# A Mamba-2 scan layer in another order, and the constant under every root moved from GpSimd to VectorE

## The chip, the cores and the metric

The kernel runs on one core of one Trainium2 chip. The metric is the device time of one execution in microseconds (us); the time of a kernel is the median of its runs. In the views of the profile PE is TensorE (matmuls), PEld its weight loads, DVE VectorE, ACT ScalarE, POOL GpSimd and SP SyncE. `L1584` is line 1584 of the kernel before.

## The reference, cut to what matters

Two layers on a sequence of 256 tokens and a model width of 1024, in float32. Each layer has a feed-forward block, a mixer and a second feed-forward block, each followed by a layer norm. The mixer of the first layer is sparse attention, that of the second a Mamba-2 scan (SSD):

```python
def layer_norm(x, g, b):
    mu = jnp.mean(xf, -1, keepdims=True)
    var = jnp.mean(jnp.square(xf - mu), -1, keepdims=True)
    return (xf - mu) * lax.rsqrt(var + LN_EPS) * g + b

def ssd_mixer(x, ...):
    z, xbc, dt = jnp.split(x @ w_in, ...)
    xbc = silu(causal_conv(xbc))                      # 4 taps
    xs, b_in, c_in = jnp.split(xbc, ...)
    dt = softplus(dt + dt_bias);  a = -exp(a_log)
    y = ssd_scan(xs, dt, a, b_in, c_in)               # 2 chunks of 128 tokens, 4 groups of 8 heads
    y = (y + xs * d_skip) * silu(z)
    y = y * lax.rsqrt(mean(square(y), per group) + RMS_EPS) * norm_g
    return y @ w_out

def ssd_scan(...):                                    # per chunk and group
    cb = einsum('bclgn,bcsgn->bcgls', cm, bm)         # C times B
    y_diag = einsum(cb * decay, xdt)                  # inside a chunk
    y_off = einsum(cm, state carried from chunk 0) * exp(a_cs)
```

Attention normalises its latent in the same way (`rms_norm` over 256 columns). So there are twelve layer-norm roots (six norms, two token tiles each), two for the latent and eight in the scan.

## The kernel before, in words

**Tiles and engines.** The 256 tokens are two token tiles t = 0, 1 of 128, which are also the two chunks of the scan. Every matmul with weights is done as three (`mm3`, L545 to L548): each operand is split into a high and a low part, and high x high, high x low and low x high are summed.

**Weights.** `Weights` (L220 on) streams the weights in units of up to 128 x 1024. SyncE loads a unit into a raw buffer (L258). `make` (L322) lets ScalarE round it to its high part (L339, with a scale L337), and `lows` (L356) lets VectorE subtract that from the raw unit for the low part (L368, with a scale L365). For six units of the scan layer the low part is made by ScalarE (L345) and an adding DMA from GpSimd's queue (L346). There are ten slots: a unit can be made while `made < done + 10`, and `free` (L410) counts a unit as done. `pump(n)` (L382) issues the low parts that are due and then makes up to n units. A raw unit is loaded when an earlier one is dead (L372).

**Order.** The program runs under a manual schedule: each engine executes its instructions in the order in which the Python code issues them, and waits by semaphore for its inputs and for buffers. So the order of the calls in `ssd` (L1618 to L1714) is the order of the work in each engine's queue.

**The scan layer up to its loop (L1618 to L1658).** `z0` and `z_half` project z, the gate; `z_half(1, 1, 0)` and `z_half(1, 1, 1)` are the two halves (over k) for group 1 and token tile 1. They sum into one PSUM bank of the pair `ptr`, free two units each, and the second half ends in a SiLU on ScalarE (L1460). `soft_a` and `soft_b` compute the softplus of dt in small GpSimd instructions, up to `adt` (L1394). Eight `bc_tile` calls project B and C. Each goes into one of three PSUM banks and through `conv`: a first tap on ScalarE (L1479), three on VectorE (L1482), and a SiLU on ScalarE (L1474), which is put off: it is issued inside the next `conv`, or by `flush()`. Behind tile 5 `cumsums` multiplies `adt` with triangles (L1402 to L1404), and `decay_load` has GpSimd's queue fetch the decay rows (L1466). Four `xs_tile` calls do the same as `bc_tile` for group 0 of x. `cb(0)`, `cb(1)` (L1504) and `cb_cross` (L1497) multiply C by B inside chunk 0, inside chunk 1 and across. `x_tok` (L1543) transposes the x tiles back to tokens (L1552), which needs the SiLU of all four.

**The loop over four groups (L1661 to L1713).** Eight pieces of other work, `f[0]` to `f[7]` (x tiles of the next group, z halves, pieces of the output product, each with a pump of one unit), are laid between the steps of the group. For token tile t the steps are `diag` (matmuls with the decay matrix, L1565), `gate` (VectorE, L1576 and L1577), `square` (ScalarE with a sum, L1581), `root`, `norm` (ScalarE scales y by the root, L1588) and `y_tr` (TensorE transposes y, L1593, and it is split). `carry` (L1569) adds to tile 1 what chunk 0 hands on: two matmuls (L1571) and two VectorE instructions (L1572, L1573). Behind the loop `tail` (L706) ends the output product, fills the slots and does the layer norm.

**Roots.** `rsqrt_pool` (L532) is called by `layernorm` (L643), `latent_norm` (L1015) and `root` (L1585). GpSimd adds the constant (L536) and raises to the power -1/2 (L538). In a root-mean-square norm a VectorE instruction ahead of it divides the sum by the width (L1584, L1014); in a layer norm VectorE's statistics (L640, L642) come ahead, and two instructions per half, centering (L649) and scaling by the root (L653), behind.

Of the kernel before, what the change touches and what calls it, by code (L numbers as in the profile page):

```python
# [13 lines left out]
ALU = mybir.AluOpType  # L14
# [10 lines left out]
KVR = 256  # L25
# [5 lines left out]
ALPHA = (2.0 * DEPTH) ** 0.25  # L31
LN_EPS = 1e-5
# [392 lines left out]
def trunk_kernel(ctx: ExitStack, tc: tile.TileContext, widths, forms, x, ln_g, ln_b, wts, kvg, convp,  # L425
# [28 lines left out]
    def tiny(s, n=32):  # L454
        return wk.tile([128, n], F32, name=nm(s), tag=f"tiny{n}", bufs=14 if n == 32 else 4)
# [73 lines left out]
    dsk = consts.tile([128, SH], F32, name="dsk")  # L529
    nc.gpsimd.dma_start(dsk, bcast_rows(d_skip, 0, SH))  # L530

    def rsqrt_pool(src, eps):  # L532

        n = src.shape[1]
        e = tiny("rse")
        nc.gpsimd.tensor_scalar(e[:, :n], src, float(eps), None, op0=ALU.add)  # L536
        o = tiny("rs")
        nc.gpsimd.tensor_tensor(o[:, :n], e[:, :n], mhalf.to_broadcast([128, n]) if n > 1 else mhalf, op=ALU.pow)  # L538
        return o[:, :n]

    def split_psum(H, L, ps):
# [77 lines left out]
    def layernorm(t, acc, c, gb, store=False, rest=None, mid=None, pre=None):  # L619

        g, b = gb
        st = tiny("st")
        x_ = xs_[t]

        def add(c0, c1, a):
            nc.vector.scalar_tensor_tensor(x_[:, c0:c1], a, c / ALPHA, x_[:, c0:c1], op0=ALU.mult, op1=ALU.add)

        w = D // 2 if rest is None else D // 4
        n = D // w
        for i in range(n):
            if i * w % 512 == 0:
                add(i * w, i * w + 512, acc[i * w // 512])
            if rest is not None and i == n - 1:
                add(i * w, D, rest)
            if pre and i == n - 1:
                pre()
            nc.vector.bn_stats(st[:, i * 6:i * 6 + 6], x_[:, i * w:(i + 1) * w])  # L640
        mv = tiny("mv", 16)
        nc.vector.bn_aggr(mv[:, :2], st[:, :6 * n].rearrange("p (a b) -> p a b", b=6))  # L642
        rstd = rsqrt_pool(mv[:, 1:2], LN_EPS / ALPHA ** 2)  # L643
        if mid:
            mid()
        hs = [slice(0, 512), slice(512, D)]

        def center(sl):
            nc.vector.scalar_tensor_tensor(x_[:, sl], x_[:, sl], mv[:, 0:1], g[:, sl],  # L649
                                           op0=ALU.subtract, op1=ALU.mult)  # L650

        def scale(sl):
            nc.vector.scalar_tensor_tensor(x_[:, sl], x_[:, sl], rstd, b[:, sl], op0=ALU.mult, op1=ALU.add)  # L653
            if store:
                nc.sync.dma_start(out[0, t * 128:(t + 1) * 128, sl], x_[:, sl])

        if store:
            for sl in hs:
                center(sl)
            for sl in hs:  # L660
                scale(sl)
        else:
            for sl in hs:
                center(sl)
                scale(sl)
# [331 lines left out]
    def attention(xT, u, ln_i):  # L997
# [13 lines left out]
            nc.scalar.activation(sq, lt[t][:, :KVR], AF.Square, accum_out=ss[t][:, 0:1])  # L1011

        def latent_norm(t):
            nc.vector.tensor_scalar(ss[t][:, 1:2], ss[t][:, 0:1], 1.0 / KVR, None, op0=ALU.mult)  # L1014
            rc = rsqrt_pool(ss[t][:, 1:2], RMS_EPS)  # L1015
            ki[t] = f1("ki")
            nc.vector.tensor_copy(ki[t][:, :128].rearrange("p (a d) -> p a d", a=2),
                                  lt[t][:, KVR + IH:NA_ATTN][:, None, :].to_broadcast([128, 2, HD]))
            wi = lt[t][:, KVR:KVR + IH]
            nc.vector.tensor_scalar(wi, wi, IH ** -0.5, None, op0=ALU.mult)  # L1020
            nc.vector.tensor_scalar(lt[t][:, :KVR], lt[t][:, :KVR], rc, None, op0=ALU.mult)
# [336 lines left out]
    def ssd(xT, u, ln_i):  # L1358
# [86 lines left out]
        def z_half(g, t, i, uu):  # L1445

            if not i:
                zps[t] = ptr() if t and g == 1 else pmm()
            ps = zps[t]
            for k in range(4 * i, 4 * i + 4):  # L1450
                H, L = W.get(uu + k // 2)
                c = slice((k % 2) * 512, (k % 2 + 1) * 512)
                sl = slice(t * 128, (t + 1) * 128)
                mm3(ps, xT.H[:, k, sl], xT.L[:, k, sl], H[:, c], L[:, c], k == 0, k == DK - 1)
                if t and k % 2:
                    W.free(uu + k // 2)
            if i:
                if not t:
                    zs[g] = f4("zs")
                nc.scalar.activation(zs[g][:, t * 512:(t + 1) * 512], ps, AF.Silu)  # L1460
# [11 lines left out]
        def flush():  # L1472
            while late:
                nc.scalar.activation(*late.pop(0), AF.Silu)  # L1474
# [22 lines left out]
        def cb_cross():  # L1497
            pt = pspare(4)
            for g in range(SG):
                nc.tensor.matmul(pt[:, g * 128:(g + 1) * 128], bT[:, g * 256:g * 256 + 128],  # L1500
                                 cTt[:, g * 256 + 128:g * 256 + 256], start=True, stop=True)
            nc.scalar.copy(cbx, pt)

        def cb(t):  # L1504
            pt = pspare(4)
            for g in range(SG):
                c = slice(g * 256 + t * 128, g * 256 + (t + 1) * 128)
                nc.tensor.matmul(pt[:, g * 128:(g + 1) * 128], bT[:, c], cTt[:, c], start=True, stop=True)
            nc.vector.tensor_mul(cbm[:, t * 512:(t + 1) * 512].rearrange("p (g l) -> p g l", g=SG),
                                 pt.rearrange("p (g l) -> p g l", g=SG),  # L1510
                                 tri[:, None, :].to_broadcast([128, SG, 128]))
# [9 lines left out]
        def decay_seg(t, g, on_act=False):  # L1521

            m = M[t, g]
            for h in range(8):
                hs = slice(h * 128, (h + 1) * 128)
                a = acs[t][:, g * 8 + h:g * 8 + h + 1]
                if on_act:
                    nc.scalar.activation(m[:, hs], m[:, hs], AF.Relu, bias=a, scale=-1.0)
                else:
                    nc.vector.tensor_scalar(m[:, hs], m[:, hs], a, 0.0, op0=ALU.subtract, op1=ALU.min)  # L1530
# [50 lines left out]
            nc.scalar.activation(xd[t], y[t], AF.Square, accum_out=ss[t][:, 0:1])  # L1581

        def root(t):
            nc.vector.tensor_scalar(ss[t][:, 1:2], ss[t][:, 0:1], 1.0 / 512, None, op0=ALU.mult)  # L1584
            ss[t] = rsqrt_pool(ss[t][:, 1:2], RMS_EPS)  # L1585

        def norm(t):
            nc.scalar.activation(y[t], y[t], AF.Copy, scale=ss[t])  # L1588
# [42 lines left out]
        s11()  # L1631
        W.pump(1)
        soft_b()
        z_half(1, 1, 0, u + 6)
        W.pump(2)
        uz = u + 6
        for i in range(8):
# [5 lines left out]
        u += 18  # L1643
        for i in range(4):
            xs_tile(0, i, u + i)
            if i == 0:
                cb_cross()
                cb(0)
                cb(1)
        decay_seg(0, 0)  # L1650
        z_half(1, 1, 1, uz)
        flush()
        x_tok(0, 0)
        x_tok(1, 0)
        decay_seg(1, 0)
# [5 lines left out]
        for g in range(SG):  # L1661
            if g < 2:
                f = [lambda i=i: xs_tile(g + 1, i, u + i) for i in range(4)]
                f += [lambda t=t, i=i: (z_half(g + 2, t, i, u + 4), W.pump(1)) for t in range(2) for i in range(2)]
            elif g == 2:
                x3 = [lambda i=i: xs_tile(3, i, u + 2 * i) for i in range(4)]
                o0 = [lambda i=i: out_piece(i, u + 2 * i + 1) for i in range(4)]
                f = [x3[0], x3[1], o0[0], x3[2], o0[1], x3[3], o0[2], o0[3]]
            else:
                f = [lambda i=i: out_piece(4 + i, u + i) for i in range(6)]  # L1670
            f[0]()
            if g:
                x_tok(0, g)
                x_tok(1, g)
            else:
                decay_cb(0, 0)
                decay_cb(1, 0)
            x_end(g)
            f[1]()
            f[2]()  # L1680
            py[0] = diag(0, g)
            gate(0, g, py[0])
            if g < 3:
                decay_load(0, g + 1)
            f[3]()
            carry(g)
            square(0)
            root(0)
            py[1] = diag(1, g)
            gate(1, g, py[1])  # L1690
            if g < 3:
                decay_load(1, g + 1)
            f[4]()
            square(1)
            root(1)
            norm(0)
            if g < 3:
                decay_seg(0, g + 1)
            f[5]()
            y_tr(0, g)  # L1700
            norm(1)
            if g < 3:
                decay_seg(1, g + 1)
                f[6]()
                flush()
                y_tr(1, g)
                decay_exp(0, g + 1)
                decay_exp(1, g + 1)
                f[7]()
                decay_cb(0, g + 1)  # L1710
                decay_cb(1, g + 1)
                W.lows()
                u += 8  # L1713
# [56 lines left out]
```

## Time and profile before

| | |
|---|---|
| time, median of 3 runs | 1024.61 us (1024.01 to 1026.11) |
| the profiled execution's own time | 1024.18 us |
| its span, first to last instruction | 1022.2 us |
| TensorE busy | 1006.5 us, 98% |
| VectorE busy | 904.0 us, 88% |
| ScalarE busy | 654.4 us, 64% |
| GpSimd busy | 110.5 us, 11% |
| HBM read, over the span | 193.48 MB, 190 GB/s |

The scan layer's own work begins at about 644 us and its loop runs from about 709 to 820 us. A row of the timeline gives the start, the length, the engine and line, the operation, what it writes and reads, a count where equal instructions follow each other, and in brackets how long the engine stood idle before and whose work ended that. A row of waits gives who waited for whom, the total, the times and the longest. A row by stretch gives for each engine the busy time and, in brackets, the instructions, then the clock granted to TensorE, the DMA share and the rate. The lines themselves stand in the prediction.

### The profile page before, as it was taken

How to read it: one execution, taken by the hardware profiler on the slowest of the kernel's cores; microseconds unless marked ns; L12 is line 12 of the kernel's file. 1: busy time of each engine (PE TensorE's matmuls, PEld its weight loads, DVE VectorE, ACT ScalarE, POOL GpSimd, SP SyncE). 2: the span in 40 equal slices, each digit the busy share in tenths (PEclk: the TensorE clock that was granted, in tenths of full speed). 3: DMA queues.
4: the chain of work that ended last, by engine and by line, in shares of the span. 5: the costliest groups of instructions: out<-in, count | busy, mean ns of one | idle time of the engine just before them, and what ended most of it. 6: DMA issues, size and time to landing. Idle time of an engine off the chain costs nothing.

```text
span 1022.2 us, 14648 instructions
## 1 busy us (share of the span) xinstructions
PE 1006.5 (98%) x5315; PEld 851.5 (83%) x5315; DVE 904.0 (88%) x1276; ACT 654.4 (64%) x947; POOL 110.5 (11%) x170
## 2 busy tenths in 40 slices
PE   8999999999999999999999999999999999999996
PEld 7888888888788888888888888999889888888885
DVE  6889997799789999988999997787899979999985
ACT  6666675477657766754867675487866645777760
POOL 2011100100011110001111000151211011010001
PEclk9999999999999999999999999999999999999998
DMA  9768998352547999792899978359765644999751
GB/s 330 291 140 285 276 319 293 120 162 88 188 143 177 267 285 280 253 326 102 209 253 294 273 256 300 129 172 258 204 211 181 216 182 111 293 290 280 220 186 41
DMA packets 63369, 226.98 MB, mean 222 GB/s; under 512 B 7136, under 2 KB 7200, under 8 KB 63296
## 3 DMA queue, kind: packets, MB, share of 16 engines
q1 hardware_dynamic: 51264, 183.43, 50.0%
q0 software_dynamic: 11744, 42.10, 20.5%
q8 instruction: 41, 0.67, 0.3%
q10 hardware_dynamic: 288, 0.52, 0.1%
q14 instruction: 32, 0.26, 0.1%
HBM read 193.48 MB, written 1.08 MB: 190 GB/s over the span
## 4 chain that ended last, share of the span: by engine, by line
PE 79%; DVE 15%; issue 3%; DMA 2%; ACT 1%; POOL 0%; POOLq 0%; DVEq 0%; SPq 0%; ACTq 0%
PE pmm L548 10%; PE pmm L547 10%; PE pmm L546 10%; PE acc L546 9%; PE acc L548 8%; PE acc L547 8%; DVE wl L368 6%; DVE raw L306 2%; PE pmm L695 2%; PE ptr L695 2%; PE ptr L547 2%; PE ptr L548 2%; PE ptr L546 2%; PE pxs L546 1%; PE pxs L548 1%
## 5 line engine op out<-in xcount | busy, mean ns | idle before, releaser
L368 DVE TENSOR_TENSOR wl<-raw,wh 128x1024 fp32r<-128x1024 f32 (+2 forms) x416 | 488.0, 1213 | 10.6 <-ACT wh L339 10.3
L339 ACT CAST wh<-raw 128x1024 fp32r<-128x1024 f32 (+2 forms) x424 | 423.9, 1044 | 109.6 <-DVE raw L306 66.7
L546 PE MATMUL acc<-wh,hH 128*128 128x512 f32 (+1 forms) x352 | 137.8, 392 | 0.0
L547 PE MATMUL acc<-wl,hH 128*128 128x512 f32 (+1 forms) x352 | 136.6, 388 | 0.0
L548 PE MATMUL acc<-wh,hL 128*128 128x512 f32 (+1 forms) x352 | 136.5, 388 | 0.0
L546 PE MATMUL pmm<-wh,xT 128*128 128x512 f32 (+2 forms) x312 | 122.6, 393 | 0.0
L548 PE MATMUL pmm<-wh,xT 128*128 128x512 f32 (+2 forms) x312 | 120.6, 386 | 0.2 <-DVE xT L543 0.2
L547 PE MATMUL pmm<-wl,xT 128*128 128x512 f32 (+2 forms) x312 | 120.0, 385 | 0.0
L279 POOL DMA_DIRECT2D raw<-raw x54 | 46.6, 863 | 397.7 <-DVE raw L306 214.2
L547 PE MATMUL pmm<-wl,xf 128*128 128x512 f32 x216 | 84.4, 391 | 0.5 <-DVE wl L368 0.3
L546 PE MATMUL pmm<-wh,xf 128*128 128x512 f32 x216 | 84.7, 392 | 0.1
L548 PE MATMUL pmm<-wh,xf 128*128 128x512 f32 x216 | 84.2, 390 | 0.0
L306 DVE TENSOR_TENSOR raw<-raw,raw 128x1024 f32<-128x1024 f32 x66 | 79.3, 1219 | 0.4
L548 PEld LDWEIGHTS acc<-wh,hL 128*128 128x128 f32 x352 | 66.1, 188 | 13.7
L547 PEld LDWEIGHTS acc<-wl,hH 128*128 128x128 f32 x352 | 66.2, 188 | 13.2 <-DVE wl L368 0.6
L546 PEld LDWEIGHTS acc<-wh,hH 128*128 128x128 f32 x352 | 66.2, 188 | 12.8
L548 PEld LDWEIGHTS pmm<-wh,xT 128*128 128x128 f32 x312 | 58.8, 189 | 13.3 <-DVE xT L543 1.6
L547 PEld LDWEIGHTS pmm<-wl,xT 128*128 128x128 f32 x312 | 59.0, 189 | 10.9 <-DVE wl L368 0.3
L546 PEld LDWEIGHTS pmm<-wh,xT 128*128 128x128 f32 x312 | 59.1, 189 | 10.4
L547 PEld LDWEIGHTS pmm<-wl,xf 128*128 128x128 f32 x216 | 40.6, 188 | 9.9 <-DVE wl L368 1.7
L546 PEld LDWEIGHTS pmm<-wh,xf 128*128 128x128 f32 x216 | 40.6, 188 | 8.6 <-ACT c L953 0.3
L548 PEld LDWEIGHTS pmm<-wh,xf 128*128 128x128 f32 x216 | 40.5, 188 | 8.4
(324 smaller groups left out, 1852.6 us busy)
## 6 DMA issues: line engine op xcount, KB each, us to landing
raw<-in_wts_dram SPq DMA_DIRECT2D x339, 512.0 KB, 5.6
raw<-raw POOLq DMA_DIRECT2D x54, 512.0 KB, 6.1
M<-scr POOLq DMA_DIRECT2D x8, 512.0 KB, 6.6
lng<-in_ln_g_dram POOLq DMA_DIRECT2D x6, 512.0 KB, 5.1
lnb<-in_ln_b_dram POOLq DMA_DIRECT2D x6, 512.0 KB, 5.2
wl<-raw POOLq DMA_DIRECT2D x6, 512.0 KB, 7.5
raw<-in_wts_dram SPq DMA_DIRECT2D x4, 408.0 KB, 6.2
out_dram<-x SPq DMA_DIRECT2D x4, 256.0 KB, 2.1
```

Source lines behind the costliest of these rows:

```text
L279: self.nc.gpsimd.dma_start(self.raw[r], self.raw[other], accum_op=ALU.add)
L306: self.nc.vector.tensor_add(self.raw[r], self.raw[r], self.raw[other])
L339: nc.scalar.copy(h[:, c:c + n], raw[:, c:c + n])
L368: self.nc.vector.tensor_sub(lo[:, s], raw[:, s], h[:, s].bitcast(F32))
L546: nc.tensor.matmul(ps, lh, rh, start=first, stop=False, skip_group_check=on)
L547: nc.tensor.matmul(ps, lh, rl, start=False, stop=False, skip_group_check=on)
L548: nc.tensor.matmul(ps, ll, rh, start=False, stop=last, skip_group_check=on)
L695: nc.tensor.matmul(ps, H[:, k * 128:(k + 1) * 128], xT.HL[:, k, :], start=k == 0, stop=False)
```

## The change

It does two things. First, the constant under the root is added by VectorE: in a root-mean-square norm as the second operation of the instruction that divides by the width, in a layer norm in an instruction of its own between the statistics and the power; GpSimd keeps the power. Second, the order of calls in the scan layer differs: the first half of z for group 1, tile 1 stands next to the second half, behind the x tiles; C times B comes behind x tile 1 with the cross product last; the put-off SiLU is flushed ahead of the second z half; in the loop `square(0)` and `root(0)` come ahead of `carry`, and `norm(0)` ahead of `f[4]` and of tile 1's square and root.

```diff
-    def rsqrt_pool(src, eps):
+    def rsqrt_pool(src):
         n = src.shape[1]
-        e = tiny("rse")
-        nc.gpsimd.tensor_scalar(e[:, :n], src, float(eps), None, op0=ALU.add)
         o = tiny("rs")
-        nc.gpsimd.tensor_tensor(o[:, :n], e[:, :n], mhalf.to_broadcast([128, n]) if n > 1 else mhalf, op=ALU.pow)
+        nc.gpsimd.tensor_tensor(o[:, :n], src, mhalf.to_broadcast([128, n]) if n > 1 else mhalf, op=ALU.pow)
...
         nc.vector.bn_aggr(mv[:, :2], st[:, :6 * n].rearrange("p (a b) -> p a b", b=6))
-        rstd = rsqrt_pool(mv[:, 1:2], LN_EPS / ALPHA ** 2)
+        nc.vector.tensor_scalar(mv[:, 2:3], mv[:, 1:2], LN_EPS / ALPHA ** 2, None, op0=ALU.add)
+        rstd = rsqrt_pool(mv[:, 2:3])
...
-            nc.vector.tensor_scalar(ss[t][:, 1:2], ss[t][:, 0:1], 1.0 / KVR, None, op0=ALU.mult)
-            rc = rsqrt_pool(ss[t][:, 1:2], RMS_EPS)
+            nc.vector.tensor_scalar(ss[t][:, 1:2], ss[t][:, 0:1], 1.0 / KVR, RMS_EPS, op0=ALU.mult, op1=ALU.add)
+            rc = rsqrt_pool(ss[t][:, 1:2])
...
-            nc.vector.tensor_scalar(ss[t][:, 1:2], ss[t][:, 0:1], 1.0 / 512, None, op0=ALU.mult)
-            ss[t] = rsqrt_pool(ss[t][:, 1:2], RMS_EPS)
+            nc.vector.tensor_scalar(ss[t][:, 1:2], ss[t][:, 0:1], 1.0 / 512, RMS_EPS, op0=ALU.mult, op1=ALU.add)
+            ss[t] = rsqrt_pool(ss[t][:, 1:2])
...
         soft_b()
-        z_half(1, 1, 0, u + 6)
         W.pump(2)
...
             xs_tile(0, i, u + i)
-            if i == 0:
-                cb_cross()
+            if i == 1:
                 cb(0)
                 cb(1)
+                cb_cross()
+        z_half(1, 1, 0, uz)
         decay_seg(0, 0)
+        flush()
         z_half(1, 1, 1, uz)
-        flush()
         x_tok(0, 0)
...
             f[3]()
-            carry(g)
             square(0)
             root(0)
+            carry(g)
             py[1] = diag(1, g)
             gate(1, g, py[1])
             if g < 3:
                 decay_load(1, g + 1)
+            norm(0)
             f[4]()
             square(1)
             root(1)
-            norm(0)
```

## The prediction

> **What bounds the kernel now.** I read the page, then busy time by stretch, then the waits, and last the timeline around each wait.
>
> ```profile
> span 1022.2 us, 14648 instructions
> PE 1006.5 (98%) x5315; PEld 851.5 (83%) x5315; DVE 904.0 (88%) x1276; ACT 654.4 (64%) x947; POOL 110.5 (11%) x170
> PE 79%; DVE 15%; issue 3%; DMA 2%; ACT 1%; POOL 0%; POOLq 0%; DVEq 0%; SPq 0%; ACTq 0%
> ...
> 683.00:710.00 27.00, 26.04 (x204) 24.59 (x203) 21.62 (x44) 21.18 (x33) 4.45 (x6) 1.00 0.79 213
> 710.00:763.00 53.00, 50.88 (x353) 46.20 (x352) 47.77 (x96) 38.22 (x56) 8.53 (x15) 1.00 0.68 206
> 763.00:1010.00 247.00, 246.78 (x1220) 206.32 (x1219) 223.74 (x288) 152.73 (x205) 23.91 (x35) 1.00 0.66 208
> ```
>
> TensorE (PE) is busy 98% of the span at a granted clock of 1.00. The change leaves every matmul in place, so it can win only where PE stands still, and must not make PE stand still elsewhere. Behind 763 PE idles 0.22 us in 247: time won before that is kept to the last matmul, with nothing left there for a late wait to hide in. From 683 to 763, the stretch that the change reorders, PE idles 0.96 + 2.12 = 3.08 us. VectorE (DVE) is busy 47.77 of 53.00 us in the scan's first two groups, so it has 5.2 us of slack there and not more. Here are PE's waits, the one at the end, and what the timeline has at each place.
>
> ```profile
> PE ptr L1593 <- ACT xdt L1588: 2.1, 2, 1.7
> DVE x L653 <- POOL rs L538: 8.3, 12, 0.8
> ...
> 299.81 0.55 PE L564 MATMUL pxT<-ident,x 128*128 128x128 f32 x3 [0.25 <-DVE x L653]
> 694.35 0.49 PE L1500 MATMUL psp<-cTt,bT 128*128 128x128 f32 x2 [0.29 <-ACT cTt L1474]
> 709.01 0.33 PE L1552 MATMUL pxt<-ident,xsT 128*128 128x128 f32 x1 [0.67 <-ACT xsT L1474]
> 731.61 0.44 PE L1593 MATMUL ptr<-ident,xdt 128*128 128x128 f32 x2 [0.43 <-ACT xdt L1588]
> 759.88 0.39 PE L547 MATMUL pmm<-wl,xT 128*128 128x512 f32 x1
> 760.10 0.39 PE L548 MATMUL pmm<-wh,xT 128*128 128x512 f32 x1
> 762.18 0.44 PE L1593 MATMUL ptr<-ident,xdt 128*128 128x128 f32 x2 [1.69 <-ACT xdt L1588]
> ```
>
> Beside 299.81, which belongs to a layer norm, there are four places: C times B waits for the SiLU of the last C tile (694.35), the first transposes of group 0 for the SiLU of the last x tile (709.01), and y's transposes in groups 0 and 1 for the normalised y (731.61, 762.18). A wait costs a little more than the idle time shown, because matmuls overlap: 762.18 - 760.10 is 2.08 us from start to start, against 0.22 for the pair before it, so 1.86 are lost where 1.69 is shown. I add the same 0.16 to each.
>
> **C times B, and the z half.** `cb_cross` comes first now and needs the tile whose SiLU is written only in the convolution just ahead of it. Behind xs tile 1, and with `cb(0)`, `cb(1)` in front, that SiLU lies a whole tile back. Gain 0.29 + 0.16 = 0.45; what hides it is the x tile's 24 matmuls.
>
> The first half of z's group 1 for token tile 1 moves from ahead of the B and C tiles to just ahead of its second half, behind the x tiles.
>
> ```profile
> 663.02 0.40 PE L546 MATMUL ptr<-wh,xT 128*128 128x512 f32 x1
> 665.76 0.28 PE L546 MATMUL pxs<-xT,wh 128*128 128x256 f32 x1
> 683.03 0.30 PE L1402 MATMUL ptr<-adt,tri 128*128 128x32 f32 x2
> 679.36 1.18 POOL L1394 TENSOR_TENSOR adt<-adt,abc 128x32 f32<-128x32 f32 x2
> 705.91 1.52 DVE L1482 SCALAR_TENSOR_TENSOR cv<-pxs,convp_sb,cv 128x255 f32<-128x255 f32 x3 [0.23 <-ACT cv L1479]
> ```
>
> Its 12 matmuls take 665.76 - 663.02 = 2.74 us. Moved, they cost nothing by themselves, but they no longer cover the softplus on GpSimd (POOL), and they newly cover the last x tile's convolution and SiLU. *Cover lost:* the B and C tiles start 2.74 us sooner, so PE comes to the cumulative sums at 680.29, while the last `adt` is ready at 679.36 + 1.18 = 680.54. The first two of those matmuls read only token tile 0, so the wait is 0 to 0.25; I take 0.1. *Cover won:* the last x tile's convolution is off DVE at 707.43 at the latest and its SiLU, now flushed ahead of z's, follows on ScalarE (ACT) directly. PE, 0.45 earlier through the gain above, reaches the fourth transpose at about 707.9 even if DVE does not move. The whole 0.67 + 0.16 = 0.83 goes; if DVE stays where it is, some 0.2 of it remains.
>
> The move also reaches the weights planner. Two of the ten slots are freed only behind the x tiles, so the pumps of the B and C tiles are cut to one unit each by the slot limit: counting `made` and `done` through the calls gives 28 units made at the loop's start in place of 30. DVE and ACT get two splits less before the loop. In the loop the splits run two units behind, six ahead of PE in place of eight, until the tail fills the slots again. One of the units so shifted into the loop has its low part made by DMA, so group 1 has one split less on DVE (a 1.21 us row, below) and ACT one pass more (about a cast, 1.04). No GpSimd or SyncE transfer is added. I put nothing on this: six units, at (683.03 - 665.76)/6 = 2.88 us of PE for a tile, are 17 us of lead, and a split takes ACT 1.04 and DVE 1.21.
>
> **Roots and norms.** In each group `root(0)` goes ahead of `carry`, and `norm(0)` ahead of `f[4]` and `square(1)`. Group 1:
>
> ```profile
> 754.65 0.69 DVE L1577 TENSOR_TENSOR xdt<-xdt,zs 128x512 f32<-128x512 f32 x1
> 756.69 1.21 DVE L368 TENSOR_TENSOR wl<-raw,wh 128x1024 fp32r<-128x1024 f32 x1
> 757.83 0.68 DVE L1572 TENSOR_TENSOR xe<-po,eacs 128x512 f32<-128x512 f32 x1
> 759.15 0.15 DVE L1584 TENSOR_SCALAR ss<-ss 128x1 f32<-128x1 f32 x1
> 759.70 0.57 POOL L538 TENSOR_TENSOR rs<-rse,mhalf 128x1 f32<-128x1 f32 x1
> 755.38 0.63 ACT L1581 ACTIVATE xtok<-xdt 128x512 f32<-128x512 f32 x1 [1.00 <-DVE xdt L1577]
> 755.92 0.18 ACT L1581 ACTIVATION_READ_ACCUMULATOR xtok<-xdt 128x1 f32 x1
> 756.01 1.04 ACT L339 CAST wh<-raw 128x1024 fp32r<-128x1024 f32 x1
> 760.79 0.63 ACT L1581 ACTIVATE xtok<-xdt 128x512 f32<-128x512 f32 x1 [3.74 <-DVE xdt L1577]
> 761.42 0.71 ACT L1588 ACTIVATE xdt<-xdt,rs 128x512 f32<-128x512 f32 x1
> 764.02 0.73 ACT L1588 ACTIVATE xdt<-xdt,rs 128x512 f32<-128x512 f32 x1
> 765.43 0.60 PE L1593 MATMUL ptr<-ident,xdt 128*128 128x128 f32 x4
> ```
>
> Today the root is ready at 760.27 and `norm(0)` still waits for `square(1)`, for which ACT idles 3.74 us. After: the sum of squares is there at 756.10, DVE reaches `root(0)` at 757.83 (the place of `carry`'s product), the power follows at about 758.0 and takes 0.57, `norm(0)` 0.71: y is ready at about 759.4, and PE asks at 760.33. The wait goes: 1.85 in group 1, and in group 0, by the same shift, 0.43 + 0.16 = 0.59. Behind the waiting `norm(0)` on ACT stand one cast (1.04) and `square(1)`; both fit into the 3.74. Behind `root(0)` on DVE stand `carry`, the gate of tile 1 and the next split; they lose 0.15 and regain it where `root(0)` stood. GpSimd's next transfer of decay rows stands behind the power and moves up with it.
>
> *What is late next* is `y_tr(1)`: PE reaches it 1.85 sooner, at 763.58, while today's `norm(1)` ends at 764.75. That loses `norm(0)` from the ACT run in front of it (0.6) and one split on DVE (1.2): about 763.0. The margin is thin, so I charge 0.15 in each of groups 0 and 1.
>
> **The constant under the root.** GpSimd's add goes in 22 places. In the ten root-mean-square places it becomes the second operation of an existing DVE instruction, which I take as free (the old one is a 0.15 us row; it can't get cheaper, and at worst costs 0.1 more, beside other work). In the twelve layer norms DVE gets one more instruction of that shape, 0.15 each. Ten of them lie beside PE's work; the one ahead of PE's wait at 299.8 and the last are felt:
>
> ```profile
> L536 POOL TENSOR_SCALAR rse<-mv x12: 773/776/1083, 179.5 to 1015.1; 128x1 f32<-128x1 f32 x12
> L536 POOL TENSOR_SCALAR rse<-ss x10: 217/220/1120, 198.1 to 816.6; 128x1 f32<-128x1 f32 x10
> 1015.04 1.42 DVE L649 SCALAR_TENSOR_TENSOR x<-x,mv,lng 128x512 f32<-128x512 f32 x2
> 1015.09 0.78 POOL L536 TENSOR_SCALAR rse<-mv 128x1 f32<-128x1 f32 x1 [6.12 <-DVE mv L642]
> 1015.95 0.93 POOL L538 TENSOR_TENSOR rs<-rse,mhalf 128x1 f32<-128x1 f32 x1
> 1016.91 1.42 DVE L653 SCALAR_TENSOR_TENSOR x<-x,rs,lnb 128x512 f32<-128x512 f32 x2 [0.46 <-POOL rs L538]
> ```
>
> Last layer norm, after: DVE's add to 1015.19, its two centerings to 1016.61; the power starts at about 1015.25 and, with its 0.93, is done by 1016.2, so the scaling starts at 1016.61 in place of 1016.91: 0.3. PE's one wait for a layer norm's scaling (L564 at 299.81, 0.25 shown, 0.41 with the overlap) shrinks by the same 0.3; its bounds are 0 and 0.41.
>
> These rows show something else: the same add takes 0.78 beside DVE's centering and 0.22 elsewhere. [...]
>
> **The sum.** 0.45 + 0.83 + 0.59 + 1.85 + 0.3 + 0.3 = 4.3, less 0.1 for `adt` and 0.3 for `y_tr(1)`: 3.9 us off the profiled execution's 1024.18 (its span and 1.98 around it). The median of the runs is 1024.61, 0.43 above it; I take the same off it: 1020.7.
>
> **Rivals.**
> [...]
>
> *PE gains, but DVE and ACT keep their old times, and the layer norms give nothing.* Then 0.25 is lost at `adt`, 0.2 at the x tile, 764.75 - 0.6 - 763.58 = 0.57 at `y_tr(1)` of group 1 plus the 0.59 by which PE came earlier from group 0, and 0.15 in group 0: 0.45 + 0.83 + 0.59 + 1.85 - 0.25 - 0.2 - 0.57 - 0.59 - 0.15 is about 2.0, time 1022.6. For it: DVE's 47.77 of 53. Against: its 5.2 us of slack, and the splits taken off it.
>
> *`root(0)` stalls DVE: slower.* It is ahead of `carry` now, so if ACT's `square(0)` is late, `carry`, the gate and the split wait, in every group. Group 3 has the least room:
>
> ```profile
> 811.66 0.19 ACT L1581 ACTIVATION_READ_ACCUMULATOR xtok<-xdt 128x1 f32 x1
> 812.20 0.69 DVE L1572 TENSOR_TENSOR xe<-pmm,eacs 128x512 f32<-128x512 f32 x1
> ```
>
> 0.35 there, 757.83 - 756.10 = 1.7 in group 1. It decides the sign once a group stalls by (3.9 + 2.05)/4 = 1.5 beyond its room, so with ACT some 2 to 3 us late, two to three casts. At 1.6 a group: 6.4 - 3.9 = 2.5, time 1027.1. Against: ACT waits for the gate at 755.38 and starts `square(0)` 0.04 behind it.
>
> **How the numbers follow.** A measurement here can tell about 0.2%, 2.05 us, from no change. Forecast 0.62 (1020.7), power shut out 0.10 (1021.6), old times kept 0.21 (1022.6, which I count as no change), stalled root 0.07 (1027.1). Faster 0.72, same 0.21, slower 0.07. The range runs from the full 4.3 on the lowest run's side (1024.61 - 4.3 - 0.6 = 1019.7) to the third case and the same scatter (1023.2); only the stalled root and the far ends are left out.
>
> **What would show it.** In the profile after: no PE wait at L1500 and L1552; L1593 without a wait on `norm` in groups 0 and 1; L1402 within 0.25 of its place; `norm(0)` ahead of `square(1)` on ACT; POOL 22 instructions fewer; scaling of the last layer norm 0.3 nearer to the statistics. I am wrong if PE waits at `y_tr(1)` by over 0.5, if DVE idles at L1584, or if PE waits for splits (wl) in the loop because of the two units.

## The result and the profile after

The changed kernel takes 1019.81 us (median of 6, 1018.72 to 1020.11) against 1024.95 us of the kernel before on the same chip (median of 6): ratio 0.9947, 95% interval 0.9934 to 0.9959. That is 5.1 us less by these medians; taken off the 1024.61 that the prediction started from, the ratio gives 1019.2. The profiled executions differ by less: 1020.11 against 1024.18, with spans of 1018.1 and 1022.2, so 4.1.

The page after, engines and chain of waits; line numbers are those of the changed kernel, one or two lower than before:

```profile
PE 1006.2 (99%) x5315; PEld 851.9 (84%) x5315; DVE 904.7 (89%) x1288; ACT 654.4 (64%) x947; POOL 102.4 (10%) x148
PE 87%; DVE 9%; issue 2%; ACT 1%; DMA 0%; DVEq 0%
```

GpSimd has its 22 instructions fewer and VectorE its 12 more; VectorE's busy time grew by 0.7 us. TensorE's busy time is the same within 0.3, and its share of the chain that ended last rose from 79% to 87%. Here are the waits of TensorE after, the whole list, and from the timeline (start, length, engine, line, operation, count, idle time before) the new wait and two places that the prediction named, the `adt` matmuls (L1401) and y's transposes in group 1 (L1592):

```profile
PE ptr L502 <- POOL ident masks.py:199: 1.4, 1, 1.4
PE pxT L562 <- DMA x<-in_x_dram: 1.1, 1, 1.1
PE pxs L544 <- ACT zs L1433: 0.4, 1, 0.4
PE pmm L545 <- DVE wl L368: 0.3, 2, 0.2
PE ptr L1085 <- DVE kiT L1038: 0.2, 1, 0.2
...
663.18 0.39 PE L544 MATMUL pxs<-xT,wh 128*128 128x256 f32 x1 [0.39 <-ACT zs L1433]
680.55 0.30 PE L1401 MATMUL ptr<-adt,tri 128*128 128x32 f32 x2
758.51 0.60 PE L1592 MATMUL ptr<-ident,xdt 128*128 128x128 f32 x4
```

The four waits of the scan are gone, and so is that for a layer norm's scaling. One is new: at 663.18 the first B tile wants a PSUM bank that a piece of z just ahead of it has filled (`z0`, group 0, token tile 1), and the SiLU that reads that piece (L1433) stands behind three casts in ScalarE's queue:

```profile
659.91 2.95 ACT L339 CAST wh<-raw 128x1024 fp32r<-128x1024 f32 x3
662.75 0.37 ACT L1433 ACTIVATE zs<-psp 128x240 f32<-128x240 f32 x1
```

By stretch (busy time and instructions of each engine, clock, DMA share, GB/s), TensorE idles 0.38 us up to 680, the wait for the bank, then not at all up to 761, and 0.21 in the 247 us behind, as before:

```profile
644.00:680.00 36.00, 35.62 (x270) 34.33 (x269) 27.44 (x39) 22.36 (x36) 15.09 (x26) 1.00 0.44 148
680.00:761.00 81.00, 81.00 (x577) 75.08 (x577) 69.33 (x142) 60.99 (x90) 11.91 (x19) 1.00 0.76 214
761.00:1008.00 247.00, 246.79 (x1226) 206.49 (x1225) 227.00 (x293) 153.52 (x205) 21.49 (x27) 1.00 0.67 211
```

Group 1 from the root on, on VectorE, GpSimd and ScalarE:

```profile
755.12 0.14 DVE L1583 TENSOR_SCALAR ss<-ss 128x1 f32<-128x1 f32 x1
755.18 0.68 DVE L1571 TENSOR_TENSOR xe<-po,eacs 128x512 f32<-128x512 f32 x1
...
755.35 0.56 POOL L536 TENSOR_TENSOR rs<-ss,mhalf 128x1 f32<-128x1 f32 x1 [9.49 <-DVE ss L1583]
...
755.94 0.73 ACT L1587 ACTIVATE xdt<-xdt,rs 128x512 f32<-128x512 f32 x1 [2.55 <-POOL rs L536]
756.57 1.04 ACT L339 CAST wh<-raw 128x1024 fp32r<-128x1024 f32 x1
758.14 0.64 ACT L1580 ACTIVATE xtok<-xdt 128x512 f32<-128x512 f32 x1 [0.53 <-DVE xdt L1576]
...
760.76 0.73 ACT L1587 ACTIVATE xdt<-xdt,rs 128x512 f32<-128x512 f32 x1
```

The root stands ahead of `carry`, `norm(0)` ahead of `square(1)`, and y of tile 0 is ready at 756.67, 1.84 us before TensorE asks for it at 758.51. Tile 1's is ready at 761.49, and TensorE does not wait for it either.

### The profile page after: what moved, and what is told of

It reads as the page before. It is cut to its first block, busy times and chain, and to the rows that moved or that the text cites. A ratio compares the mean times of both kernels' runs of the same rounds, so it can differ in the third digit from the quotient of the medians.

```text
span 1018.1 us, 14629 instructions
## 1 busy us (share of the span) xinstructions
PE 1006.2 (99%) x5315; PEld 851.9 (84%) x5315; DVE 904.7 (89%) x1288; ACT 654.4 (64%) x947; POOL 102.4 (10%) x148
## 4 chain that ended last, share of the span: by engine, by line
PE 87%; DVE 9%; issue 2%; ACT 1%; DMA 0%; DVEq 0%
PE pmm L545 11%; PE pmm L546 11%; PE pmm L544 11%; PE acc L544 9%; PE acc L546 9%; PE acc L545 9%; DVE wl L368 5%; PE pmm L694 2%; PE ptr L694 2%; PE ptr L545 2%; DVE raw L306 2%; PE ptr L546 2%; PE ptr L544 2%; PE pxs L544 2%; PE pxs L545 2%
## 5 line engine op out<-in xcount | busy, mean ns | idle before, releaser
L544 PE MATMUL acc<-wh,hH 128*128 128x512 f32 (+1 forms) x352 | 137.8, 392 | 0.0
L544 PE MATMUL pmm<-wh,xT 128*128 128x512 f32 (+2 forms) x312 | 122.8, 394 | 0.0
L544 PE MATMUL pmm<-wh,xf 128*128 128x512 f32 x216 | 84.7, 392 | 0.0
L544 PEld LDWEIGHTS acc<-wh,hH 128*128 128x128 f32 x352 | 66.2, 188 | 12.8
L544 PEld LDWEIGHTS pmm<-wh,xT 128*128 128x128 f32 x312 | 59.1, 189 | 10.5
L544 PEld LDWEIGHTS pmm<-wh,xf 128*128 128x128 f32 x216 | 40.5, 188 | 8.6 <-ACT c L952 0.3
```

What stands on the lines that cost most here:

```text
L544: nc.tensor.matmul(ps, lh, rh, start=first, stop=False, skip_group_check=on)
```

## The experiments

Every ratio is to the kernel before on the same chip; the spans are those of the profiled execution. Spans of single executions are to be read with care: already in the first 20 us, ahead of everything that the change touches, they differ. The matmul that starts at 21.23 in the first profile of before starts 0.59 earlier in r2, 0.71 in r4 and 0.50 in r12, and 0.36 later in r5. Where the text gives what a part of the program wins, by the starts of the same matmuls, this is taken off.

| run | what it is | median us | ratio (95%) | span us |
|---|---|---|---|---|
| r1 | before | 1025.33 | 1.0006 (0.9996 to 1.0015) | 1022.2 |
| r2 | constant alone | 1022.73 | 0.9983 (0.9975 to 0.9992) | 1020.0 |
| r3 | loop's order alone | 1022.86 | 0.9985 (0.9977 to 0.9994) | 1021.6 |
| r4 | order ahead of the loop alone | 1022.98 | 0.9989 (0.9980 to 0.9998) | 1020.5 |
| r5 | after | 1019.78 | 0.9948 (0.9936 to 0.9961) | 1018.1 |
| r6 | loop's order, two units fewer | 1022.20 | 0.9974 (0.9964 to 0.9985) | 1020.8 |
| r7 | all but z's half | 1020.67 | 0.9959 (0.9945 to 0.9973) | 1018.5 |
| r8 | after, banks begun elsewhere | 1019.81 | 0.9952 (0.9940 to 0.9965) | 1017.4 |
| r9 | r7 with two units fewer | 1020.25 | 0.9957 (0.9944 to 0.9970) | 1020.8 |
| r10 | after, `norm(0)` put back | 1020.91 | 0.9959 (0.9947 to 0.9971) | 1019.1 |
| r11 | after, `root(0)` put back | 1020.77 | 0.9957 (0.9944 to 0.9970) | 1019.1 |
| r12 | before | 1024.65 | 0.9999 (0.9989 to 1.0010) | 1021.6 |
| r13 | before, wait made longer | 1026.62 | 1.0013 (1.0004 to 1.0022) | 1022.8 |
| r14 | r9 again | 1020.66 | 0.9963 (0.9950 to 0.9975) | 1021.1 |
| r15 | after | 1019.29 | 0.9947 (0.9934 to 0.9959) | 1018.0 |

**The two kernels again** (r1, r5, r15; no edit).

> The kernel before, unchanged, as a measure of what runs of one kernel differ by. Scatter theory: its ratio to the kernel before is 1.000 with an interval of some 0.0015 to either side, its runs spread over 1 to 2 us, and its profile has the same four PE waits in the scan (0.29, 0.67, 0.43, 1.69 us, each within 0.1). Rival, that the profile before was a lucky one and a typical execution loses 1 us more in the scan: the second profile shows a PE wait larger by 0.5 us or more.

> The changed kernel, unchanged, timed again over more runs. Trace theory: the two profiles differ by 4.1 us, so the ratio to the kernel before is about 0.996. Rival: the first medians, 5.1 us apart, were right and the profiles missed 1 us; ratio 0.9947 again.

> The changed kernel itself, beside the two others on the same chip (the earlier run of this purpose held the kernel before). Profiled execution 1019.9 to 1020.2, spans 1016.8 to 1018.1, ratio to the kernel before 0.9947; no execution with a mean clock of 0.996, since no wait behind the start is longer than 0.4.

Both kernels repeat, and so do the four waits of before. That the medians lie further apart (4.7 in r5, 5.6 in r15) than the profiles (4.1) repeats as well, and r13 below bears on a part of it.

The run r12 was meant to hold the changed kernel but held the kernel before, so what was expected of it does not apply:

> The changed kernel itself, beside the three others on the same chip. Profiled execution 1019.9 to 1020.2 with a span of 1018.1, ratio to the kernel before 0.9947 as in its two earlier measurements; the scale on which the others are read. If the kernel with the z half kept and two units fewer is better, it lies 0.5 to 0.9 below this one.

It gives one more measurement of the kernel before, 1024.65, with its four waits.

**The parts alone** (r2, r3, r4). r2 is the diff's `rsqrt_pool` and its three callers; r3 its hunk in the loop; r4 its hunks ahead of the loop.

> Only the constant under the roots on VectorE, the order of before. Sum theory: the positions of the matmuls give 0.5 us up to the scan layer and the end of the last layer norm 0.47 us, so 0.9 to 1.0 us less than before (ratio about 0.999), and the PE waits for y's transposes shrink by 0.1 to 0.3 us each at most. Rival, that the faster roots are the main gain: 2 us or more less, with the waits at the transposes of y (0.43 and 1.69 before) halved.

> Only the order inside the loop over groups: square(0) and root(0) ahead of carry, norm(0) ahead of f[4]; the constant stays on GpSimd, the head of the scan as before. Sum theory: both waits of PE for y's transposes go (0.59 and 1.85 us), 2.4 us less than before (ratio about 0.9976), and no wait appears at the transposes of tile 1. Rival, that the waits go to the transposes of tile 1, 3 us later: PE waits of 0.5 us or more there, 1.2 us or less gained.

> Only the order ahead of the loop: z half moved, C times B behind x tile 1, the early flush. Sum theory: 0.45 and 0.83 us won, 0.55 us lost at the first B tile, which waits for a PSUM bank: 0.7 us less than before (ratio about 0.9993), and the waits at y's transposes stay (0.43 and 1.69, within 0.3). Rival, that the two weight units made later are what relieves VectorE in group 1: the 1.69 us wait shrinks by 1 us or more and the gain is 1.7 us or more.

Waits in the scan that are left, in r2, then in r3, which also keeps r2's two ahead of the loop (0.7 and 0.3), then in r4:

```profile
PE ptr L1592 <- ACT xdt L1587: 2.0, 2, 1.6
PE pxt L1551 <- ACT xsT L1473: 0.7, 1, 0.7
PE psp L1499 <- ACT cTt L1473: 0.3, 1, 0.3
```

```profile
PE ptr L1593 <- ACT xdt L1588: 1.1, 1, 1.1
```

```profile
PE ptr L1593 <- ACT xdt L1588: 0.9, 2, 0.5
PE acc L546 <- DVE xtok L1555: 0.5, 1, 0.5
PE pxs L546 <- ACT zs L1434: 0.4, 1, 0.4
```

The constant touches no wait of the scan by more than 0.1; what it wins lies at the layer norms. Its span is 2.2 shorter than before; without the 0.59 at the start that is 1.6, more than the 0.9 to 1.0 expected. The loop's order alone does not give the 2.4 of the sum: the two waits for tile 0 go, and one of 1.1 us comes up at 764.27, which is `y_tr(1)` of group 1, the thing named as late next. By the starts of the same matmuls it nets about 0.75. The order ahead of the loop, which touches no norm, cuts the wait of group 1 from 1.7 to 0.5, as r4's rival had it; it brings the wait for the bank, and one in which a matmul of the output product waits for `x_tok` of the next group. Within the scan the parts alone give about 0.35, 0.75 and 0.9, together 2.0; the whole change gives 3.25. So one part needs another.

**Which part it needs** (r6, r7). r6 is r3 with two units fewer made ahead of the loop, r7 the whole change with z's half left ahead of the B tiles, so that 30 units are made as before:

```diff
r6, on r3:
-            W.pump(1 + i % 2)
+            W.pump(1)
r7, on after:
+        z_half(1, 1, 0, u + 6)
         W.pump(2)
...
-        z_half(1, 1, 0, uz)
```

> The loop's order alone (constant and head as before), and beside it the pump of every B and C tile cut to one unit, so that 28 units are made at the loop's start as in the changed kernel, with nothing else of the head moved. Split theory: the wait of 1.08 us at the transposes of tile 1 in group 1, which the loop's order alone had, goes to under 0.2, because one split less stands on VectorE ahead of that group's gates; 1.9 to 2.2 us less than before. Rival, that it is the z half's new place or the earlier start of the loop that takes this wait away: the 1.08 stays within 0.3 and the gain stays near 0.8 us.

> All of the change but the z half, which stays ahead of the B tiles. Split theory: no wait at the first B tile, 0 to 0.3 us at the first transposes of group 0, but the planner is back at 30 units and a wait of 0.8 to 1.2 us stands at the transposes of tile 1 in group 1; 1 us or more slower than the changed kernel by the positions of the matmuls. Rival: the wait at tile 1 stays away and the kernel is 0.3 us or more faster than the changed one, for want of the 0.55 at the bank.

In r6 TensorE waits nowhere in the loop for y: the two units fewer took the 1.1 away. (Its span is 1.4 less than before, or 1.7 without the 0.29 that it loses in the first 20 us; 1.9 to 2.2 were expected, and C times B waits 0.45 there in place of 0.29.) In r7, with 30 units, the 1.1 is back, though all else of the change is there:

```profile
PE ptr L1592 <- ACT xdt L1587: 1.1, 1, 1.1
```

That shows the link. A unit that is made two positions later leaves group 1 with one split less on VectorE (1.21 us), and `norm(1)` hangs on VectorE there. Without it the loop's new order only moves the wait from tile 0 to tile 1.

**The new wait** (r8). On the changed kernel the B, C and x tiles begin with another of their three banks:

```diff
-        zps, turn = {}, [0]
+        zps, turn = {}, [2]
```

> The changed kernel, with the three PSUM banks of the B, C and x tiles taken in another turn, so that the first B tile gets the bank that the dt product of tile 0 left and not the one whose SiLU is still queued on ScalarE. Bank theory: the wait of 0.39 us shown (0.55 from start to start) ahead of the first B tile goes and 0.5 us is won, none given back later. Rival: the B tile then waits as long for its weights' low part or for the next bank.

The wait at L544 is gone and the one the prediction priced at 0 to 0.25 shows in its place. TensorE and GpSimd there:

```profile
679.83 0.41 PE L1401 MATMUL ptr<-adt,tri 128*128 128x32 f32 x2
...
678.70 1.28 POOL L1393 TENSOR_TENSOR adt<-adt,abc 128x32 f32<-128x32 f32 x2
```

The matmul starts 0.42 behind its neighbour's start at 679.41, where 0.12 is usual: 0.3. The span is 0.7 shorter, of which 0.24 lie in the first 20 us; the time is not shorter: 0.9952 against 0.9948 beside it.

**The loop's order, line by line** (r10, r11), on the changed kernel:

```diff
r10:
-            norm(0)
             f[4]()
             square(1)
             root(1)
+            norm(0)
r11:
+            carry(g)
             square(0)
             root(0)
-            carry(g)
```

> The changed kernel with one line back: norm(0) behind root(1) again, root(0) still ahead of carry. If the early norm(0) is what removed the waits for y_tr(0), and the early root(0) only serves it: norm(0) stands behind square(1) on ACT again, waits for y_tr(0) return in groups 0 and 1, but by less than the 0.43 and 1.71 of the kernel before because the two units made later take one split off DVE in group 1: about 0.2 and 0.5 (as in the run of the head alone), span 0.7 to 1.2 above the changed kernel's 1018.1. Rival, that with one split less the order of the norms no longer matters: no wait, span 1018.1. If the waits are back at their full size: span 1020.2 or more.

> The changed kernel with carry ahead of square(0) and root(0) again, norm(0) still early. root(0) then stands behind carry's product on DVE (0.68) and behind the split ahead of that, so the root comes about 0.7 later in each group. If only norm(0)'s place matters: y is still ready before PE asks, no wait at L1592, span 1018.1 within 0.2. If root(0)'s place carries part of the gain: ACT waits longer ahead of norm(0), square(1) behind it starts later, and a wait of 0.3 to 1 at y_tr(0) or y_tr(1) of group 1 shows, span 1018.4 to 1019.1. The prediction's rival that root(0) ahead of carry stalls DVE would make this kernel quicker than the changed one.

Waits for y in r10, then in r11:

```profile
PE ptr L1592 <- ACT xdt L1587: 1.0, 2, 0.5
```

```profile
PE ptr L1592 <- ACT xdt L1587: 0.6, 1, 0.6
```

Each line put back costs 1.0 of span. In r10 tile 0 waits in groups 0 and 1 (730.28 and 759.63), as expected. In r11 it is tile 1 of group 1 that waits (762.55): the root comes 1.65 later (756.77 against 755.12) and stands behind `carry` whole, and with it `norm(0)`, a cast, `square(1)` and `norm(1)` are all later on ScalarE. So the "only the norm matters" theory fell, and `root(0)` ahead of `carry` is worth about 1, not a stall.

**A better order?** (r9, r14; the same kernel twice). r7 with r6's edit has neither the wait for the bank nor, by the reasoning above, that for `y_tr(1)`.

> All of the change except that z's half stays ahead of the B tiles, and the second pump of that stretch is cut to one unit, so that 28 units are made at the loop's start as in the changed kernel. If the waits are the sum of what the runs so far showed: no wait for the PSUM bank (0.55 less than the changed kernel), none for adt, and, unlike the run with the z half kept and 30 units, no wait for y_tr(1) in group 1 (1.1 there): span 1017.3 to 1017.6, 0.5 to 0.8 below the changed kernel's 1018.1, ratio to the kernel before about 0.994. Rival, that the two units were not what removed the wait for y_tr(1) but the moved z half itself: that wait is back with about 1.1 at L1592 and the span is 1018.5 or more.

> The kernel with the z half kept and two units fewer once more, because in its profiled execution VectorE stood still for 4.36 us ahead of the tile products of C and B. If that was one execution's accident: span 1017.2 to 1018.0, no wait of over 0.3 behind the start, and the time 0 to 0.8 below that of the changed kernel on the same chip. If it belongs to the kernel: the same idle time and a span near 1020.8 again.

The wait for `y_tr(1)` is indeed absent, but both profiled executions have something that no other kernel shows. VectorE in r9, then in r14, and two more rows of r9:

```profile
703.19 0.69 DVE L1508 TENSOR_TENSOR cbm<-psp,tri 128x512 f32<-128x512 f32 x1 [4.36 <-issue]
```

```profile
703.59 0.69 DVE L1508 TENSOR_TENSOR cbm<-psp,tri 128x512 f32<-128x512 f32 x1 [4.62 <-issue]
```

```profile
L1508 DVEq EVENT_SEMAPHORE  x1: 5809/5809/5809, 697.3 to 697.3; - x1
693.29 0.90 POOL L346 DMA_DIRECT2D wl<-raw  x1 [1.92 <-ACT wl L345]
```

VectorE stands still for 4.4 and 4.6 us ahead of the same instruction, the product of C and B with the triangle (L1508), and TensorE then waits 2.0 and 2.2 us at the transposes of the x tiles. The timeline puts the idle time down to "issue", which names no engine. But VectorE's queue stands at a semaphore of L1508 for 5.81 us, from 697.34 on, and by the trace it is waiting there for two transfers. One is the load of a raw unit, which landed long before, at 674.70. The other is the adding transfer of L346, which makes a low part: GpSimd issued it at 693.29, it landed at 703.11, and VectorE goes on at 703.19. In r14 it landed at 703.51, and VectorE goes on at 703.59. Raw units and `cbm`, which L1508 writes, come out of the same twelve buffers (`f4`), so most likely `cbm` got the buffer of the raw unit that this transfer was still reading; the trace does not name the buffer. In the profile of the changed kernel L1508 waits for no transfer.

The executions behind the first, which have no profile here, have spans of 1017.2 to 1018.3 in r9 and 1018.0 to 1019.1 in r14, against 1017.2 to 1017.6 for the same executions of the changed kernel in r15. They are 2.0 to 3.6 us shorter than the profiled ones, so they can hardly have the whole of this wait. No version here is better than the changed kernel.

**Where the rest of the gain comes from** (r13). Each execution's result lists its span and mean granted clock. Of 76 executions of the kernel before beside these runs, 23 have a clock of 0.996 and a mean span of 1024.2; the 53 others (0.997, 0.998) have 1022.3. The 22 of r1 and r12 divide in the same way, 6 and 16. The three profiles of before all have 0.997. Of 16 executions of the changed kernel none has 0.996. Whether this low clock hangs on the wait of 1.7 us for y is the question of r13, the kernel before with that wait made longer:

```diff
             square(1)
+            if g == 1:
+                square(1)
             root(1)
```

> The kernel before with square(1) of group 1 done twice, so that ACT is 0.6 to 0.8 later at norm(0) and the wait for y_tr(0) of group 1 grows from 1.7 to 2.3 to 2.5. [...] Rival, that the low clock comes by chance and has nothing to do with the wait: a third at 0.996 as before, spans 0.6 to 0.8 above those of the kernel before in both groups.

In its profiled execution the wait for y grew as meant:

```profile
PE ptr L1593 <- ACT xdt L1588: 2.8, 2, 2.3
```

Of its 11 executions 8 have a clock of 0.995 or 0.996 and a mean span of 1025.1, and 3 have 0.997 and 1023.0. The share went from 23 of 76 to 8 of 11 by one longer wait. If the two had the same chance of a low clock, 8 or more of the 11 would be low about once in a hundred times, so the chance rival is unlikely, though not excluded.

In the profile of before the clock is 1.00 up to 1013.6 us, where TensorE's work ends, and in that of r13 it is 1.00 around the wait. In the profile of r9 it falls, behind the wait of 2.0 us, and r14, with its wait of 2.2, has the same mean clock, 0.996, in its profiled execution, where its other four have 0.997 and 0.998. Here are rows by stretch of r9, then matmuls of one shape ahead of the wait and behind it, then the stretch with the wait in r13 and the two behind it:

```profile
706.30:709.70 3.40, 1.43 (x11) 1.06 (x11) 3.33 (x11) 2.12 (x5) 0.00 (x0) 1.00 1.00 245
709.70:713.10 3.40, 3.40 (x18) 3.40 (x18) 3.40 (x10) 2.12 (x2) 0.00 (x0) 0.51 0.54 181
713.10:716.50 3.40, 3.40 (x30) 3.40 (x29) 2.92 (x8) 2.46 (x3) 0.00 (x0) 0.99 0.00 0
```

```profile
698.42 0.28 PE L544 MATMUL pxs<-xT,wh 128*128 128x256 f32 x1
698.54 0.28 PE L545 MATMUL pxs<-xT,wh 128*128 128x256 f32 x1
...
710.81 0.41 PE L544 MATMUL pxs<-xT,wh 128*128 128x256 f32 x1
711.02 0.41 PE L545 MATMUL pxs<-xT,wh 128*128 128x256 f32 x1
```

```profile
760.00:763.00 3.00, 0.67 (x5) 0.29 (x4) 2.58 (x7) 2.40 (x6) 1.17 (x4) 1.00 0.66 178
763.00:767.00 4.00, 4.00 (x23) 3.36 (x22) 4.00 (x15) 3.92 (x7) 0.32 (x1) 1.00 1.00 336
767.00:771.00 4.00, 4.00 (x27) 3.59 (x26) 4.00 (x5) 3.95 (x5) 0.00 (x0) 1.00 0.63 225
```

In r9 the matmuls follow each other every 0.12 us ahead of the wait and every 0.21 behind it. For 3.4 us the clock is at a half (0.51), which costs 3.4 x 0.49 = 1.7 us on top of the wait, close to the 1.9 between the two groups of spans of before. It takes 1.7/1022 = 0.0016 off the mean clock, about the step from 0.998 to 0.996.

Which waits lower the clock is not settled; their length alone does not tell. In r9 it fell behind 2.0 us, and in the profiled execution of r13 it stayed at 1.00 in and behind 2.3. The waits of 1.6 in r2 and r12 did not lower it either (1.00 in every stretch from 758 to 770 us), and none of the 11 executions of r2 has 0.996. That the low executions of before owe their clock to the wait of 1.7 has the share in r13 for it and r2 against it; it is not shown.

## Why the prediction was right and wrong

The direction and the mechanism held: the waits went for the reasons given, and 3.9 were forecast where 4.1 came between the profiled executions. That these two numbers lie so close is partly luck, because errors cancel: 0.55 at the PSUM bank was not foreseen, while the norms gave 0.42 more than forecast and the 0.4 charged at `adt` and `y_tr(1)` did not come. By the sum's terms (starts of the same matmuls, idle time with overlap):

| term | forecast | measured |
|---|---|---|
| C times B | 0.45 | 0.45 |
| `x_tok` | 0.83 | 0.83 |
| `y_tr(0)`, groups 0 and 1 | 0.59 + 1.85 | 0.60 + 1.83 |
| layer norms that TensorE waits for | 0.3 | 0.55 |
| last layer norm | 0.3 | 0.47 |
| `adt` | -0.1 | 0 |
| `y_tr(1)`, 0.15 twice | -0.3 | 0 |
| the PSUM bank at 663.18 | not seen | -0.55 |

The measured column adds up to 4.2; the changed kernel's profile is 0.14 later than that of before at 21 us, which leaves the 4.1 of the profiled executions.

*Layer norms.* I counted the one row with an idle time in the waits; three scalings had been felt a little (0.26, 0.11 and 0.18 won at 187, 300 and 468 us).

*The last layer norm.* VectorE and GpSimd, after:

```profile
1010.64 0.43 DVE L638 BATCH_NORM_STATS2 st<-x 128x6 f32<-128x256 f32 x1
1011.48 1.40 DVE L648 SCALAR_TENSOR_TENSOR x<-x,mv,lng 128x512 f32<-128x512 f32 x2
1012.80 1.41 DVE L652 SCALAR_TENSOR_TENSOR x<-x,rs,lnb 128x512 f32<-128x512 f32 x2
...
1011.64 0.98 POOL L536 TENSOR_TENSOR rs<-mv,mhalf 128x1 f32<-128x1 f32 x1 [6.91 <-DVE mv L641]
```

From the last statistics to the scaling it is 12.80 - 10.64 = 2.16, against 16.91 - 14.28 = 2.63 before, whose row is this:

```profile
1014.28 0.43 DVE L640 BATCH_NORM_STATS2 st<-x 128x6 f32<-128x256 f32 x1
```

The power ends at 1012.62, within the second centering (which ends at 1012.88). The case of 1021.6, "power shut out", to which the prediction gave 0.10, has it start only behind both centerings; no run shows that. In the profiles after and of r2 it starts 0.16 behind the first centering's start (1011.64 after) and takes 0.98, against 0.56 in group 1.

*The bank.* "Moved, they cost nothing by themselves" failed. The moved half's 12 matmuls had covered the three casts and the SiLU of `z0`; I looked for the cover lost at the softplus, 17 us later, and not at the bank that the next tile takes over. That wait in turn covers `adt`: taken away in r8, `adt` shows with 0.3.

*The planner.* "I put nothing on this" was right for the lead of the splits and wrong for the loop. The two units are what makes `y_tr(1)` of group 1 ready in time; r3 and r7, with 30 units, wait 1.1 there, and r6, with 28, does not. The working had "one split on DVE (1.2)" in it as a help to a thin margin; it is the margin. The rival of old times kept put this wait at 0.57 + 0.59, which is what r3 and r7 have.

*The stalled root* did not come: VectorE does not idle ahead of L1583 in group 1, and r11 shows that the old place costs 1.0.

*The step that put the time below the range* is "The median of the runs is 1024.61, 0.43 above it; I take the same off it", and with it the low end "1024.61 - 4.3 - 0.6". It takes what one profiled execution wins as what every execution wins. The range ended at 1019.7; the 1019.2 that the ratio gives lies 0.5 below it. The profiles differ by 4.1, the ratio is worth 5.4, and the sum has no term for the 1.3 between them. About 0.6 of it is the lower clock: 23 of 76 executions of before have it and are 1.9 longer, 0.3 x 1.9 = 0.6 on average, and no execution of the changed kernel has it. That the wait of 1.7 is what lowers it there has r13 for it and is not shown. Another 0.6 is that the changed kernel's profiled executions, the first of each run, have spans of 1018.0 to 1018.1, while the mean of all 16 is 1017.5. All three start slowly, 0.13 to 0.36 later at 21 us than the first profile of before, which can be a part of it; the rest stays open.

## What to carry to other kernels

A wait that is taken away can move to whatever is late next on the same engines, as in r3 (1.1 us at `y_tr(1)`): price the pair, here the order of the norms and the split that had to leave VectorE, since neither gave its part alone. When work is moved from between two users of a PSUM bank, look at what stands in the queue ahead of the bank's reader. Set the end of a range from many executions with their spans and clocks, because one profile shows a wait only at the price that it had that time.

## What the runs showed of the hardware

Behind a TensorE wait of 2.0 us in r9 the granted clock was at a half for 3.4 us (0.51 from 709.70 to 713.10), and matmuls of one shape followed each other every 0.21 us in place of 0.12; that cost 1.7 us on top of the wait. In the 3.4 us ahead of that TensorE had been busy for 1.43. In r14, with a wait of 2.2 us, the mean clock was 0.996 as in r9. With waits of 2.3 us (r13), 1.7 (before) and 1.6 (r2, r12) the clock stayed at 1.00 behind them in the profiled executions. What made the difference is not shown.

A second arithmetic operation in VectorE's 128x1 instruction cost nothing here: L1583 took 0.146 us in the median of 8, and L1584 of the kernel before, with a single operation, took the same.
